# Scores of a head pair in two steps over four PSUM banks instead of three, and the sample's steps moved within the attention stage

## The chip, the cores and the metric

The kernel runs on one core of one Trainium2 chip. The metric is the device time in microseconds (us) of one execution. The engines are TensorE (PE: matmuls and transposes; PEld its weight loads), VectorE (DVE), ScalarE (ACT), GpSimd (POOL) and SyncE (SP), which issues the DMAs.

## The reference

One step of a two-layer encoder for two groups of tokens that share the weights: a prompt of 512 tokens and a sample of 32, so 544 columns in all. A layer projects its input by `W_in`, runs three branches (band attention, retention, a gated recurrence called RG-LRU), merges them by gates, adds a per-layer embedding and ends in a LayerNorm. What the change touches is the attention of the prompt and of the sample, 8 heads of 64. With 512 tokens in chunks of 64 and 8 chunks of look-back every frame sees its own chunk and all before it:

```python
scores = einsum('bcqhd,bckhd->bhcqk', qc * d**-0.5, kp)   # own chunk and 8 before
scores = scores + rel_bias(table, qpos, kpos)              # per head, by clipped distance
scores = where(valid, scores, NEG_INF)
probs  = softmax(scores)
out    = einsum('bhcqk,bckhd->bcqhd', probs, vp)
ya     = out * silu(za)
```

The sample's 32 tokens attend to a cache of 256 keys and to themselves, with the same bias table.

## The kernel before

Activations lie feature by token: 128 features on the partitions, 544 tokens along the row. All projections are streams of blocks: one block is a 128x128 piece of a weight times 544 columns. To keep fp32 accuracy in a faster format each weight and each input is split into a high and a low part (`wh`, `wl`, `xh`, `xl`), and a block (`block`, L248) is three products, each of 288 and 256 columns: six matmuls at L256. The splits are made by ACT (L211) and DVE (L212) from weights that SP loads (L203) into three buffers.

Everything else is done in the gaps between blocks. The order is written out by hand: each side job is a generator; `tick` (L174) runs ahead of each block, issues weight splits that are due (`stream`) and resumes every job whose time has come; a job says by `yield n` in how many blocks it goes on. The table `PACE` (L70) holds these numbers. So a number in `PACE` moves all instructions of a job, on every engine, and each engine then runs its instructions strictly in the order issued.

Attention's part of this, once for each layer:

- `attn_job` (L366) waits until the value transposes, the recurrence's gates and the first key tile are there, and then goes through four pairs of heads. For each pair it loads two bias tables (`bias_loads`, SP, L347), masks a corner on POOL (L379), and starts three steps, eight blocks apart: query tiles (0, 1), then (2,), then (3,).
- `attn_step` (L394) for query tile i has (i + 1) * 128 keys. Two heads of the pair, j = 0 and 1, lie on partitions 0 to 63 and 64 to 127, and their matmuls (L407, 64 rows, three products) write two PSUM banks, `sc`. `exps` (L355) adds the bias and takes the row's maximum on DVE (L357) and exponentials with their sums on ACT (L359); `norm` (L362) divides on DVE (L363, L364). Between these stand `at1` (3), `at1` and `at2` (2) blocks. Then for each head the tile `sx` is transposed on TensorE into the one `tp` bank (L423) and ACT copies it into `PT` (L429); `at3` is 3 blocks.
- `attn_pv` (L436) multiplies the transposed probabilities by the values into the one `pv` bank (L441, 64 columns of the array for each head), and DVE copies the result (L443). It is kept in a list that `flush` (L390) empties: in the next pair's step (0, 1), behind its first transposes, or after the last pair.
- `sample_job` (L454) loads the cache and eight pieces of bias (`sb`, L458) as soon as the last key tile is there, waits 11 blocks, and does the sample's scores (L468), transposes (L481) and values (L494) four, four and three blocks apart.
- At the same time run the recurrence's last scans (DVE L555, POOL L553) in the first pair, the evacuation of new query, key and later-branch tiles from the projections' two `mm` banks (ACT L866, L264, L890; DVE L265, L891), and in the third and fourth pair the rotation of retention's keys: four DMAs on SP copy halves into `swap` (L567, L568), DVE and POOL multiply and add (L570 to L577).

PSUM has eight banks: `mm` takes two buffers of two banks, `sc` two, `tp` and `pv` one each. Small tiles, `sx`, `sb`, `bias` and `swap` among them, share a ring of 14 buffers (`tmp`).

## Time and profile before

| | |
|---|---|
| median of 3 runs | 1309.28 us (1309.03 to 1309.94) |
| the profiled execution's own time | 1310.85 us |
| its span, first to last instruction | 1309.1 us |
| TensorE's mean granted clock | 0.997 |
| TensorE busy | 1291.6 us (99%) |
| DVE, ACT, POOL busy | 718.8, 547.2, 175.8 us |
| score matmuls (L407) on the chain that ended last | 2% of the span |
| values matmuls (L441), transposes (L423) on it | 1% each |

Attention's stage lasts from 96.7 us to some 211 us in the first layer and from 745.4 us to some 860 us in the second. Between 96.7 and 107.2 us DVE is busy for 9.6 of 10.5 us and ACT for 6.6; between 119.6 and 145.3 us DVE for 14.9 of 25.7. A row of the timeline gives start, duration, engine, line, instruction, shapes and count; what the engine waited for ahead of it, if it idled, stands in brackets at its end. Ends of matmuls are modelled, so a cost on TensorE is read from one start to another.

### The profile page before, as it was taken

The page shows a single profiled execution, that of the slowest core. Times are in us where ns is not written, and L with a number is a line of the kernel's source. Part 1 is how long each engine was busy: PE and PEld are TensorE (multiplying, and loading weights), DVE is VectorE, ACT ScalarE, POOL GpSimd, SP SyncE. Part 2 cuts the span into 40 slices and gives each one's busy share as a digit, 9 for nine tenths or more (in the row PEclk, how much of TensorE's full clock was granted, in tenths as well). Part 3 has the DMA queues.
Part 4 walks back from the last instruction along what each step waited for, and adds up shares of the span by engine and source line. Part 5 has one row for each costly group of instructions (what it writes and reads, how often), then busy time and mean ns, then how long its engine had stood idle before and what let it go on. Part 6 is the DMA issues. An engine that isn't in the chain of part 4 may idle for free.

```text
span 1309.1 us, 25085 instructions
## 1 busy us (share of the span) xinstructions
PE 1291.6 (99%) x10550; PEld 1257.1 (96%) x10550; DVE 718.8 (55%) x1272; ACT 547.2 (42%) x1082; POOL 175.8 (13%) x158
## 2 busy tenths in 40 slices
PE   9999999999999999999999999999999999999996
PEld 9999889999999999999989998999999999999996
DVE  5657663573754453465584766626637434434567
ACT  5665544323632233333276655443235322332231
POOL 0110120410101201000032102224001011010000
PEclk9999999999999999999999999999999999999998
DMA  7433522231222222424122345222222222224231
GB/s 263 153 128 100 173 66 82 84 104 49 85 93 82 97 73 90 165 98 146 65 104 79 120 109 166 74 82 82 90 65 81 96 82 84 94 81 166 81 113 69
DMA packets 44609, 134.80 MB, mean 103 GB/s; under 512 B 9488, under 2 KB 11792, under 8 KB 42704
## 3 DMA queue, kind: packets, MB, share of 16 engines
q1 hardware_dynamic: 44496, 133.20, 30.5%
q8 instruction: 83, 1.36, 0.4%
q14 instruction: 30, 0.25, 0.1%
HBM read 117.02 MB, written 11.70 MB: 98 GB/s over the span
## 4 chain that ended last, share of the span: by engine, by line
PE 95%; DVE 3%; DMA 1%; ACT 1%; issue 0%; SPq 0%; POOL 0%; DVEq 0%
PE mm L256 84%; PE sc L407 2%; PE pv L441 1%; PE tp L423 1%; PE tp L334 1%; PE sc L667 1%; PE pv L690 1%; PE pv L522 0%; DVE r L819 0%; PE sc L522 0%; DVE xl L265 0%; PE sc L750 0%; PE sc L603 0%; PE pv L685 0%; DMA raw<-in_W 0%; PE sc L494 0%
## 5 line engine op out<-in xcount | busy, mean ns | idle before, releaser
L256 PE MATMUL mm<-xh,wh 128*128 128x288 f32 x2144 | 455.5, 294 | 0.4 <-ACT xrp L900 0.4
L256 PE MATMUL mm<-xh,wl 128*128 128x288 f32 x2144 | 444.0, 288 | 0.0
L256 PE MATMUL mm<-xl,wh 128*128 128x288 f32 x2144 | 442.7, 288 | 0.0
L212 DVE TENSOR_TENSOR wl<-raw,wh 128x512 fp32r<-128x512 f32 (+1 forms) x354 | 261.3, 756 | 282.2 <-ACT wh L211 278.3
L256 PEld LDWEIGHTS mm<-xh,wh 128*128 128x128 f32 x2144 | 328.4, 189 | 10.8 <-issue 7.5
L256 PEld LDWEIGHTS mm<-xl,wh 128*128 128x128 f32 x2144 | 328.7, 188 | 0.0
L256 PEld LDWEIGHTS mm<-xh,wl 128*128 128x128 f32 x2144 | 328.5, 188 | 0.0
L211 ACT CAST wh<-raw 128x512 fp32r<-128x512 f32 (+1 forms) x354 | 208.2, 614 | 34.2 <-PE mm L256 30.8
L922 ACT ACTIVATE sg<-mm 128x544 f32<-128x544 f32 x48 | 30.0, 625 | 154.0 <-PE mm L256 153.9
L934 POOL TENSOR_TENSOR m<-m,sg 128x544 f32<-128x544 f32 x30 | 46.8, 1561 | 316.7 <-DVE sg L932 316.7
L359 ACT ACTIVATE sx<-sx,sst 128x128 f32<-128x128 f32 (+4 forms) x68 | 38.0, 559 | 65.5 <-DVE sst L357 58.6
L256 PE MATMUL mm<-xh,held 128*128 128x288 f32 (+1 forms) x320 | 64.0, 292 | 0.3 <-ACT ple L942 0.3
L256 PE MATMUL mm<-mh,wh 128*128 128x288 f32 (+1 forms) x256 | 53.0, 288 | 0.0
L256 PE MATMUL mm<-mh,wl 128*128 128x288 f32 (+1 forms) x256 | 53.0, 288 | 0.0
L256 PE MATMUL mm<-ml,wh 128*128 128x288 f32 (+1 forms) x256 | 52.8, 287 | 0.0
L256 PEld LDWEIGHTS mm<-xh,held 128*128 128x128 f32 x320 | 51.3, 188 | 0.6 <-ACT ple L942 0.5
L256 PE MATMUL mm<-xl,held 128*128 128x288 f32 (+1 forms) x160 | 46.3, 290 | 0.6 <-DVE xl L265 0.6
L264 ACT CAST xh<-r 128x544 fp32r<-128x544 f32 (+2 forms) x32 | 17.0, 532 | 68.3 <-DVE r L952 64.1
L932 DVE TENSOR_TENSOR sg<-mm,sg 128x544 f32<-128x544 f32 x32 | 23.2, 725 | 37.1 <-PE mm L256 37.1
L913 ACT ACTIVATE z<-mm 128x544 f32<-128x544 f32 x24 | 15.0, 626 | 59.6 <-PE mm L256 59.6
L571 POOL TENSOR_TENSOR swap<-swap,cst 128x544 f32<-128x544 f32 x16 | 25.3, 1579 | 108.4 <-DMA swap<-QB 32.1
L256 PEld LDWEIGHTS mm<-mh,wh 128*128 128x128 f32 x256 | 39.4, 188 | 0.0
(251 smaller groups left out, 1785.2 us busy)
## 6 DMA issues: line engine op xcount, KB each, us to landing
raw<-in_W SPq DMA_DIRECT2D x189, 512.0 KB, 3.3
pled<-ple SPq DMA_DIRECT2D x4, 1088.0 KB, 9.0
ple<-pled SPq DMA_DIRECT2D x4, 1088.0 KB, 6.8
bias<-in_RB SPq DMA_DIRECT2D x16, 256.0 KB, 3.8
x<-in_xT SPq DMA_DIRECT2D x4, 544.0 KB, 9.3
o_v<-VA SPq DMA_DIRECT2D x2, 1088.0 KB, 4.6
o_k<-KT SPq DMA_DIRECT2D x2, 1088.0 KB, 5.1
swap<-KB SPq DMA_DIRECT2D x32, 68.0 KB, 2.0
```

The source lines that it names most:

```text
L211: S.copy(h[:, k:k + step], t)
L212: V.tensor_tensor(lo[:, k:k + step], t, h[:, k:k + step].bitcast(F32), SUB)
L256: T.matmul(ps[:, MM0 + a:MM0 + b], lhsT=w[:, n % 4, :], rhs=x[:, a:b], start=first and i == 0, stop=last and i == 2)
L264: S.copy(h, src)
L334: T.transpose(tp[:rows, t * 128:(t + 1) * 128], src[:, t, c0:c0 + rows], ident)
L359: S.activation(x, x, AF.Exp, bias=s[:, 0:1], scale=-1.0, accum_out=s[:, 1:2])
L407: T.matmul(scs[j][:, o:o + n], lhsT=q_[r, p, i * 128:i * 128 + 128], rhs=k_[r, p, :n], start=k == 0, stop=k == 2)
L571: G.tensor_tensor(sw, sw, cst[:, C_SIN:C_SIN + N], MUL)
L913: S.activation(z, pv, AF.Sigmoid)
L922: S.activation(sg, pv, AF.Sigmoid)
L932: V.tensor_tensor(sg, pv, sg, MUL)
L934: (V if kind == "bB" and t == 7 else G).tensor_tensor(m, m, sg, ADD)
```

## The change

The steps of a pair are (3, 1) and (2, 0), 11 and 13 blocks apart (24 blocks a pair as before). Step (3, 1) is the wide one: the scores of query tile 3 go to the two `sc` banks, those of tile 1 to the `tp` bank (first head) and the `pv` bank (second head). Its probabilities lie in three `sx` tiles, one for each head's 512 columns and one that both heads share with 256 columns each, so it has three groups of four transposes. Step (2, 0) keeps both of its tiles in the `sc` banks, 384 + 128 columns, and has two groups of four. The values of the pair before are flushed behind the wide step's first transposes; the next pair's bias loads stand at the second step. After the last step 3 blocks pass (`attn_end`), where it was 9. The sample's bias pieces are loaded 12 blocks later than its cache, and its first scores 12 blocks after that.

```diff
-    "va0": 5, "va": 3, "step": 8, "attn_end": 9, ... "sample": 11, ...
+    "va0": 5, "va": 3, "step": (11, 13), "attn_end": 3, ... "sample": 12, ...
@@ attn_job
-                for qs in ((0, 1), (2,), (3,)):
-                    if qs[0] == 2 and p < 3:
+                for n, qs in enumerate(((3, 1), (2, 0))):
+                    if n and p < 3:
                         bias_loads(p + 1)
                     add(attn_step(p, qs))
-                    yield PACE["step"]
+                    yield PACE["step"][n]
@@ attn_step
-            scs, xs, todo = [psum("sc") for _ in range(2)], [], []
-            o = 0
+            wide = qs[0] == 3
+            scs, xs = [psum("sc") for _ in range(2)], [tmp("sx", (128, 512)) for _ in range(2)]
+            at_ = {(qs[0], j): (scs[j], xs[j], 0) for j in range(2)}
+            if wide:
+                x = tmp("sx", (128, 512))
+                at_.update({(qs[1], j): (psum(("tp", "pv")[j]), x, 256 * j) for j in range(2)})
+            else:
+                at_.update({(qs[1], j): (scs[j], xs[j], 128 * (qs[0] + 1)) for j in range(2)})
...
-                        T.matmul(scs[j][:, o:o + n], lhsT=q_[r, p, i * 128:i * 128 + 128], rhs=k_[r, p, :n],
+                        sc, x, o = at_[i, j]
+                        o *= not wide
+                        T.matmul(sc[:, o:o + n], lhsT=q_[r, p, i * 128:i * 128 + 128], rhs=k_[r, p, :n],
                                  start=k == 0, stop=k == 2)
...
-            for j in range(2):
+            for x in xs + ([at_[1, 0][1]] if wide else []):
                 tp = psum("tp")
-                for c in range(0, o, 128):
-                    T.transpose(tp[:, c:c + 128], xs[j][:, c:c + 128], ident)
-                if j == 0 and qs[0] == 0:
+                mine = sorted((o, i, j) for (i, j), (_, y, o) in at_.items() if y is x)
+                end = mine[-1][0] + 128 * (mine[-1][1] + 1)
+                for c in range(0, end, 128):
+                    T.transpose(tp[:, c:c + 128], x[:, c:c + 128], ident)
+                if wide and x is xs[0]:
                     flush()
-                for i in qs:
+                for c, i, j in mine:
                     copy("p%d" % j)(env["PT"][j][:, :i + 1, i * 128:i * 128 + 128],
                                     tp[:, c:c + 128 * (i + 1)].rearrange("p (a b) -> p a b", b=128))
-                    c += 128 * (i + 1)
+                if not wide and x is xs[1]:
+                    env["pvs"].append(lambda: attn_pv(p))
                 yield PACE["at3"]
-            if qs[-1] == 3:
-                env["pvs"].append(lambda: attn_pv(p))
@@ sample_job
             ks, vc = sample_loads()
+            while "ya" not in env:
+                yield 2
+            yield PACE["sample"]
             sb = [tmp("sb", (128, PAST + NS)) for _ in range(2)]
             for h in range(8):
                 Q.dma_start(out=sb[h % 2][32 * (h // 2):32 * (h // 2) + 32],
                             in_=RB[l, h, 0:NS, 128:128 + PAST + NS])
-            while "ya" not in env:
-                yield 2
-            yield PACE["sample"]
+            yield 12
```

How this moves instructions is shown at three places. TensorE, the first step of the first pair of heads: `sc`, `tp` and `pv` ahead of the arrow are the banks written, `KTh`, `KTl`, `QTh`, `QTl` the high and low parts of keys and queries. Before:

```order
684 L256 MATMUL mm<-xh,wl 128x256
685 L407 MATMUL sc<-KTh,QTh 128x128 x2
686 L407 MATMUL sc<-KTh,QTl 128x128 x2
687 L407 MATMUL sc<-KTl,QTh 128x128 x2
688 L407 MATMUL sc<-KTh,QTh 128x256 x2
689 L407 MATMUL sc<-KTh,QTl 128x256 x2
690 L407 MATMUL sc<-KTl,QTh 128x256 x2
691 L256 MATMUL mm<-xh,wh 128x288
```

and now:

```order
684 L256 MATMUL mm<-xh,wl 128x256
685 L414 MATMUL sc<-KTh,QTh 128x512 x2
686 L414 MATMUL sc<-KTh,QTl 128x512 x2
687 L414 MATMUL sc<-KTl,QTh 128x512 x2
688 L414 MATMUL tp<-KTh,QTh 128x256
689 L414 MATMUL pv<-KTh,QTh 128x256
690 L414 MATMUL tp<-KTh,QTl 128x256
691 L414 MATMUL pv<-KTh,QTl 128x256
692 L414 MATMUL tp<-KTl,QTh 128x256
693 L414 MATMUL pv<-KTl,QTh 128x256
694 L256 MATMUL mm<-xh,wh 128x288
```

The step holds 512 + 256 columns a head in place of 128 + 256, and the smaller group is written to the other two banks.

TensorE again, where the values of the first pair are multiplied, in the second pair's time. Before:

```order
900 L256 MATMUL mm<-xh,wl 128x256
901 L423 MATMUL tp<-cst,sx 128x128 x3
902 L441 MATMUL pv<-PT,vatok 64x512 x2
903 L441 MATMUL pv<-PT,vatok 64x384 x2
904 L441 MATMUL pv<-PT,vatok 64x256 x2
905 L441 MATMUL pv<-PT,vatok 64x128 x2
906 L407 MATMUL sc<-KTh,QTh 128x384 x2
907 L407 MATMUL sc<-KTh,QTl 128x384 x2
908 L407 MATMUL sc<-KTl,QTh 128x384 x2
909 L256 MATMUL mm<-xh,wh 128x288
```

and now:

```order
905 L256 MATMUL mm<-xh,wl 128x256
906 L434 MATMUL tp<-cst,sx 128x128 x4
907 L450 MATMUL pv<-PT,vatok 64x512 x2
908 L450 MATMUL pv<-PT,vatok 64x384 x2
909 L450 MATMUL pv<-PT,vatok 64x256 x2
910 L450 MATMUL pv<-PT,vatok 64x128 x2
911 L256 MATMUL mm<-xh,wh 128x288
```

Step (2,)'s scores stood right behind the values; now projection blocks do, and the scores of step (2, 0) come three blocks later, behind the wide step's second transposes.

ACT, from the exponentials of the first pair's first step to its copies of transposed probabilities. Before:

```order
118 L359 ACT_TABLE_LOAD
119 L359 ACTIVATE sx,sst<-sx,sst 128x128
120 L359 ACTIVATE sx,sst<-sx,sst 128x256
121 L211 CAST wh<-raw 128x512
122 L359 ACTIVATE sx,sst<-sx,sst 128x128
123 L359 ACTIVATE sx,sst<-sx,sst 128x256
124 L866 COPY KT<-mm 128x544
125 L264 CAST KTh<-KT 128x544
126 L211 CAST wh<-raw 128x512
127 L429 COPY PT<-tp 128x128
128 L429 COPY PT<-tp 128x2x128
129 L359 ACTIVATE sx,sst<-sx,sst 128x384
```

and now:

```order
118 L359 ACT_TABLE_LOAD
119 L359 ACTIVATE sx,sst<-sx,sst 128x512
120 L359 ACTIVATE sx,sst<-sx,sst 128x256
121 L211 CAST wh<-raw 128x512
122 L359 ACTIVATE sx,sst<-sx,sst 128x512
123 L359 ACTIVATE sx,sst<-sx,sst 128x256
124 L876 COPY KT<-mm 128x544
125 L264 CAST KTh<-KT 128x544
126 L211 CAST wh<-raw 128x512
127 L439 COPY PT<-tp 128x4x128
128 L211 CAST wh<-raw 128x512
129 L439 COPY PT<-tp 128x4x128
```

The order of kinds is the same up to the first copy; two exponentials have grown from 128 to 512 columns, and one copy of 512 stands for two of 128 and 256. DVE's order in this stretch changes in the same way. On SP the eight `sb` loads of a layer, which stood ahead of the first key tile's four `swap` copies, now stand behind these and the next weight load, ahead of the second key tile's four; the last pair's `bias` loads, which stood ahead of those four, now stand behind them.

More of the change, by code (lines that the diff above doesn't have):

```diff
@@ L395, in attn_step @@
             QTh, QTl, KTh, KTl = (env[k] for k in ("QTh", "QTl", "KTh", "KTl"))
-            scs, xs, todo = [psum("sc") for _ in range(2)], [], []
-            o = 0
+            wide = qs[0] == 3
[6 more added lines that the diff above has]
+                at_.update({(qs[1], j): (scs[j], xs[j], 128 * (qs[0] + 1)) for j in range(2)})
             now = [], []
-            for j in range(2):
-                xs.append(tmp("sx", (128, 512)))
             for i in qs:
@@ L406, in attn_step @@
                         r = slice(64 * j, 64 * j + 64)
-                        T.matmul(scs[j][:, o:o + n], lhsT=q_[r, p, i * 128:i * 128 + 128], rhs=k_[r, p, :n],
+                        sc, x, o = at_[i, j]
+                        o *= not wide
+                        T.matmul(sc[:, o:o + n], lhsT=q_[r, p, i * 128:i * 128 + 128], rhs=k_[r, p, :n],
                                  start=k == 0, stop=k == 2)
                 for j in range(2):
-                    now[j].append((xs[j][:, o:o + n], scs[j][:, o:o + n], env["bias", p, j][:, 512 - n:]))
-                o += n
+                    sc, x, o = at_[i, j]
+                    c = 0 if wide else o
+                    now[j].append((x[:, o:o + n], sc[:, c:c + n], env["bias", p, j][:, 512 - n:]))
+            todo = []
             for j in range(2):
@@ L419, in attn_step @@
             yield PACE["at2"]
-            for j in range(2):
+            for x in xs + ([at_[1, 0][1]] if wide else []):
                 tp = psum("tp")
-                for c in range(0, o, 128):
-                    T.transpose(tp[:, c:c + 128], xs[j][:, c:c + 128], ident)
-                if j == 0 and qs[0] == 0:
+                mine = sorted((o, i, j) for (i, j), (_, y, o) in at_.items() if y is x)
[3 more added lines that the diff above has]
+                if wide and x is xs[0]:
                     flush()
-                c = 0
-                for i in qs:
+                for c, i, j in mine:
                     copy("p%d" % j)(env["PT"][j][:, :i + 1, i * 128:i * 128 + 128],
                                     tp[:, c:c + 128 * (i + 1)].rearrange("p (a b) -> p a b", b=128))
-                    c += 128 * (i + 1)
+                if not wide and x is xs[1]:
+                    env["pvs"].append(lambda: attn_pv(p))
                 yield PACE["at3"]
-            if qs[-1] == 3:
-                env["pvs"].append(lambda: attn_pv(p))
         def attn_pv(p):
```

2 rows, old and new, of the table PACE are left out of this document.

## The prediction

> **What bounds the kernel now.** I read the page first, then the chain, then what TensorE waited for. In the page, busy times:
>
> ```profile
> PE 1291.6 (99%) x10550; PEld 1257.1 (96%) x10550; DVE 718.8 (55%) x1272; ACT 547.2 (42%) x1082; POOL 175.8 (13%) x158
> ...
> PE 95%; DVE 3%; DMA 1%; ACT 1%; issue 0%; SPq 0%; POOL 0%; DVEq 0%
> ```
>
> TensorE is busy from end to end, and the chain that ended last runs 95% through it. So only two things can move the end: what TensorE itself spends on the attention steps, and time in which it is made to wait. Its waits, first and last of 8 groups:
>
> ```profile
> PE tp L750 <- DVE r L968: 2.0, 2, 1.4
> ...
> PE mm L256 <- ACT phl L264: 0.2, 1, 0.2
> ```
>
> The eight add up to 7.8 us, and none of them lies in attention (95 to 211 us, and 744 to 860 us for the second layer). No wait is there to be removed; the change can gain only in TensorE's own time.
>
> What a score step costs is read from start to start, since ends are modelled. A row of the timeline is start, duration, instruction. First the step (0,1), then steps (2,) and (3,), each behind three transposes, and between them three transposes alone:
>
> ```profile
> 96.40 0.41 PE L256 MATMUL mm<-xh,wl 128*128 128x288 f32 x2
> ...
> 97.02 0.27 PE L407 MATMUL sc<-KTl,QTh 64*128 64x128 f32 x2
> 97.13 0.34 PE L407 MATMUL sc<-KTh,QTh 64*128 64x256 f32 x2
> 97.30 0.28 PE L407 MATMUL sc<-KTh,QTl 64*128 64x256 f32 x2
> 97.42 0.28 PE L407 MATMUL sc<-KTl,QTh 64*128 64x256 f32 x2
> ...
> 97.99 0.41 PE L256 MATMUL mm<-xl,wh 128*128 128x288 f32 x2
> ...
> 103.51 0.42 PE L256 MATMUL mm<-xh,wl 128*128 128x288 f32 x2
> ...
> 105.27 0.41 PE L256 MATMUL mm<-xl,wh 128*128 128x288 f32 x2
> ...
> 107.01 0.41 PE L256 MATMUL mm<-xh,wl 128*128 128x288 f32 x2
> ...
> 107.84 0.41 PE L256 MATMUL mm<-xl,wh 128*128 128x288 f32 x2
> ...
> 111.12 0.42 PE L256 MATMUL mm<-xh,wl 128*128 128x288 f32 x2
> ...
> 113.06 0.41 PE L256 MATMUL mm<-xl,wh 128*128 128x288 f32 x2
> ```
>
> From 97.99 to 103.51 stand 22 pairs of projection matmuls: 5.52 / 22 = 0.251 us a pair, 0.753 us a block of three. Each stretch above holds two such pairs, so 0.50 is taken off. (0,1): 1.59 - 0.50 = 1.09. Three transposes: 0.83 - 0.50 = 0.33, or 0.11 each. (2,): 1.76 - 0.50 - 0.33 = 0.93. (3,): 1.94 - 0.50 - 0.33 = 1.11. A pair of heads pays 3.13 us for scores.
>
> **The scores, two steps for three.** The matmuls stay the same in number and shape; groups are joined. A group that comes second in a step costs only its own starts: for 256 columns 0.17 (97.13 to 97.30), 0.12, and 0.12 again; for 128 columns 0.17 and twice 0.11 (97.02 to 97.13). So step (3,1) is 1.11 + 0.41 = 1.52, step (2,0) is 0.93 + 0.39 = 1.32, together 2.84: 0.29 less in the first pair of heads. If the first start of a joined group is no dearer than its others, it is 0.40 less; if a group in another bank saves nothing, zero. I take 0.29, the rows' own value.
>
> In the later pairs the old step (2,) stood directly behind the probabilities-times-values matmuls, and in the new order projection matmuls follow those. What the neighbourhood was worth:
>
> ```profile
> 126.91 0.42 PE L256 MATMUL mm<-xh,wl 128*128 128x288 f32 x2
> ...
> 130.97 0.42 PE L256 MATMUL mm<-xl,wh 128*128 128x288 f32 x2
> ...
> 207.78 0.41 PE L256 MATMUL mm<-xh,wl 128*128 128x288 f32 x2
> ...
> 210.79 0.41 PE L256 MATMUL mm<-xl,wh 128*128 128x288 f32 x2
> ```
>
> The first stretch holds three transposes, the pv group and step (2,): 4.06 - 0.50 - 0.33 = 3.23. The second holds the pv group alone: 3.01 - 0.50 = 2.51. Side by side the score step cost 0.72 instead of 0.93, and this 0.21 is given up in three of four pairs. A layer saves 4 x 0.29 - 3 x 0.21 = 0.53 us, two layers **1.1 us** (with 0.40 and otherwise the same 1.9; with zero it loses 1.3).
>
> By the Trainium skill, TensorEngine Tiling (Array Packing), Key Properties, it is the change of tiling mode, not of tile, that drains the engine; its page TensorE: Matmul & The Clock Gate, Step-by-step, puts a drain at about 128 cycles, 0.053 us as an estimate. The new order has ten changes of mode fewer, which would be worth 0.5 us, where the rows give 0.1 a change and 1.1 in all; that the gain goes by changes of mode agrees with the rows, the page's price is half of theirs.
>
> Transposes stay 20 a pair, in five groups instead of six; at 0.11 each and nothing by group this is zero. The sample's matmuls are the same, spread anew: zero, or 0.1 a layer either way for one score group that now stands before transposes.
>
> **The new wait.** The wide step's first two transpose groups stand three blocks apart with nothing but blocks between, and share the one tp bank. ACT must empty it in that time. In the first pair of each layer ACT and DVE are late, because DVE still scans for the recurrence:
>
> ```profile
> 99.34 1.36 POOL L553 TENSOR_TENSOR lru_r<-lru_r,lru_i 128x544 f32<-128x544 f32 x1
> 99.41 2.37 DVE L555 TENSOR_TENSOR_SCAN lru_i<-lru_a,lru_r 128x512 f32<-128x512 f32 x1
> ...
> 102.65 0.29 DVE L364 TENSOR_SCALAR sx<-sx,sst 128x128 f32<-128x128 f32 x1
> ...
> 103.31 0.28 DVE L357 CUSTOM_DVE_ANT_0 sx<-sc,bias 128x128 f32<-128x128 f32 x1
> ...
> 104.04 0.49 ACT L359 ACTIVATE sx<-sx,sst 128x256 f32<-128x256 f32 x1
> ...
> 106.23 0.53 ACT L429 COPY PT<-tp 128x128 f32<-128x128 f32 x2
> ...
> 107.26 0.49 PE L423 MATMUL tp<-cst,sx 128*128 128x128 f32 x3
> ...
> 114.36 0.68 DVE L357 CUSTOM_DVE_ANT_0 sx<-sc,bias 128x512 f32<-128x512 f32 x1
> ...
> 115.08 0.72 ACT L359 ACTIVATE sx<-sx,sst 128x512 f32<-128x512 f32 x1 [0.99 <-DVE sst L357]
> ...
> 115.80 0.60 ACT L211 CAST wh<-raw 128x512 fp32r<-128x512 f32 x1
> ...
> 119.47 0.49 DVE L364 TENSOR_SCALAR sx<-sx,sst 128x512 f32<-128x512 f32 x1
> ...
> 120.85 0.58 ACT L429 COPY PT<-tp 128x512 f32<-128x512 f32 x1
> ...
> 747.74 1.37 POOL L553 TENSOR_TENSOR lru_r<-lru_r,lru_i 128x544 f32<-128x544 f32 x1
> 748.10 2.08 DVE L555 TENSOR_TENSOR_SCAN lru_i<-lru_a,lru_r 128x512 f32<-128x512 f32 x1
> ...
> 754.63 0.53 ACT L429 COPY PT<-tp 128x128 f32<-128x128 f32 x2
> ...
> 755.94 0.49 PE L423 MATMUL tp<-cst,sx 128*128 128x128 f32 x3
> ```
>
> Old order: ACT's copies end at 106.76 and the next group starts at 107.26, 0.50 to spare. New order, step by step. The first head's score instructions take about 0.4 longer (512 columns for 128), but the scan behind them ended 1.08 and 1.07 us after POOL's end in the two layers, however long after POOL's start it began; so its end stays. The norm grows by 0.49 - 0.29 = 0.20: the second head's 512 scores start at 103.51. Its exponential starts 0.72 later (114.36 to 115.08), at 104.23, and the next one 0.72 after that, at 104.95, where 104.04 stood: 0.91 late. Key copy, cast and weight cast follow as before, so the PT copy starts at 106.23 + 0.91 = 107.14 and, with 512 columns, ends at 107.72. TensorE meanwhile comes earlier: 107.26 less three transposes and step (2,) between (0.33 + 0.93), plus the longer first step (0.43) and four transposes (0.44): 106.87. It **waits 0.85 us**. In the second layer the copy ends at 754.63 + 0.91 + 0.58 = 756.12 and TensorE comes at 755.55: 0.57. Together **1.4 us**. If the scan's end moved with its start this would be 2.2; if ACT kept the old times, zero. I take 1.4, since the end held in both layers.
>
> Later places have cover. In pairs two to four the pv group (2.3 us) lies between the first two transpose groups. The wide step's own matmuls into the tp bank start two blocks and the 512 columns (1.5 + 0.7) after the narrow step's last transposes, whose copies need some 0.8.
>
> **Moved DMAs.** The sample's eight bias loads now stand on SP ahead of the second key tile's four swaps, and one pair's bias loads behind them:
>
> ```profile
> 139.77 5.86 SPq L458 DMA_DIRECT2D sb<-in_RB  x8
> ...
> 151.14 0.35 SPq L203 DMA_DIRECT2D raw<-in_W  x1
> ...
> 155.91 0.51 SPq L567 DMA_DIRECT2D swap<-KB  x1
> ...
> 162.56 1.61 DVE L570 TENSOR_TENSOR KB<-KB,cst 128x544 f32<-128x544 f32 x1
> ```
>
> Behind that raw load they end at 151.5 + 5.9 = 157.4, so the swaps leave up to 1.5 us late. Behind the waiting DVE rotation (L570) are queued the narrow step's norms, for which transposes wait that stand eight blocks (6 us) after its scores. That covers it; uncovered it costs one rotation, 1.6 us a layer. Weight loads keep their times. I take zero.
>
> **Sum.** -1.1 + 1.4 = +0.3 us. The profiled execution, 1310.85 us with a span of 1309.1, would be 1311.15 (span 1309.4). It lay 1.57 above the runs' median of 1309.28, so that median becomes **1309.6**. The likeliest case's own range, gain 1.0 to 1.9 and wait 0.8 to 2.2, is 1308.2 to 1310.5.
>
> **Rivals.** *No wait*: ACT is in time and the gain stands, 1309.28 - 1.1 = 1308.2 (1307.4 with 1.9). For it speaks the old 0.50 to spare, against it the 0.91. *The tp bank is late everywhere*: if in pairs two to four the copies end as late as in the first (over 2.2 us after the transposes, from where it decides), the wide step waits inside its scores. The first pair's copies ended 2.5 us after theirs (103.51 + 0.25 + the 0.49 of such a group, 104.25, to 106.76), 512 columns would add 0.2: 0.5 each in six places, 1309.6 + 3.0 = 1312.6, slower. Against it: without the scan nothing holds ACT up there. It goes by the Trainium skill's Perfetto Trace Analysis, Matmuls, which asks that independent groups rotate through different banks so that emptying overlaps. *Joining saves a step's whole fixed cost*: 1.09 less three starts of 0.11 and three of 0.12 leaves 0.40; eight of these, the neighbourhood kept and no wait: -3.2, 1306.1, faster. Against it: the 0.17 of the second group and the 3.23.
>
> **Chances.** Forecast 0.58, no wait 0.22, late everywhere 0.12, whole fixed cost 0.05, other small differences 0.03. A measurement of this kernel can tell about 0.2%, 2.6 us. Only "late everywhere" and a tail of lost cover lie above it (0.14), only the last rival and a little of "no wait" below (0.06); 0.80 is no change. The range, 1307.4 to 1312.0, holds the first two cases with their bounds and leaves out most of the other two.
>
> **What would show it.** Right: in the first pair of each layer a TensorE wait of 0.5 to 1.0 us at the second transpose group, on ACT's PT copy; steps of 1.52 and 1.32 us; pv followed by blocks at 2.5. Wrong: no wait there, or one at the wide step's tp matmuls, at the sample's scores, or on DVE for KB behind a swap; a joined group that starts at other intervals in another bank.

## The result, and the profile after

The change made the kernel slower: 1319.14 us median of 6 runs (1316.42 to 1320.59) against 1308.49 (1307.13 to 1309.94), ratio 1.0074, 95% interval 1.0063 to 1.0085. The forecast was 1309.6 with a range to 1312.0, and it gave 0.80 to no change that a measurement can tell. The measured median lies 7.1 us above the range, and the loss of 0.74% is clear of the noise. The profiled execution took 1319.89 us with a span of 1318.0, 8.9 more than before.

The page of the changed kernel, busy times and the chain that ended last:

```profile
PE 1295.1 (98%) x10550; PEld 1260.1 (96%) x10550; DVE 709.7 (54%) x1272; ACT 542.7 (41%) x1082; POOL 174.9 (13%) x158
...
PE 86%; DVE 7%; ACT 4%; issue 2%; DMA 1%; DVEq 0%; POOL 0%; SPq 0%; ACTq 0%
```

TensorE's share of the chain fell from 95 to 86%: DVE and ACT now set the pace in places. What TensorE waited for (us in all, times, longest), the three groups that did not exist before:

```profile
PE tp L434 <- ACT PT L494: 4.4, 2, 2.3
...
PE tp L434 <- ACT PT L439: 1.3, 2, 0.7
...
PE tp L334 <- ACT VB L876: 0.7, 2, 0.4
```

The second was forecast; the first, which is the largest, was not. L494 is the sample's copy of its transposed probabilities. The place is the fourth pair's wide step. Rows of the timeline (start, duration, instruction, idle time before it and who ended it):

```profile
172.47 0.41 PE L256 MATMUL mm<-xh,wl 128*128 128x288 f32 x2
172.81 0.50 PE L414 MATMUL sc<-KTh,QTh 64*128 64x512 f32 x2
...
174.43 0.41 PE L256 MATMUL mm<-xl,wh 128*128 128x288 f32 x2
...
178.56 1.36 POOL L581 TENSOR_TENSOR swap<-swap,cst 128x544 f32<-128x544 f32 x1
178.60 1.60 DVE L364 TENSOR_SCALAR sx<-sx,sst 128x512 f32<-128x512 f32 x1
179.02 0.49 PE L491 MATMUL tp<-cst,sx 128*128 128x128 f32 x3
180.61 0.41 PE L256 MATMUL mm<-xh,wl 128*128 128x288 f32 x2
180.78 0.69 DVE L357 CUSTOM_DVE_ANT_0 sx<-sc,bias 128x512 f32<-128x512 f32 x1
181.56 0.72 ACT L359 ACTIVATE sx<-sx,sst 128x512 f32<-128x512 f32 x1 [3.64 <-issue]
182.28 0.49 ACT L359 ACTIVATE sx<-sx,sst 128x256 f32<-128x256 f32 x1
182.78 0.35 ACT L493 COPY PT<-tp 128x256 f32<-128x256 f32 x1
183.03 0.25 ACT L494 COPY PT<-tp 32x128 f32<-32x128 f32 x1
183.33 0.66 PE L434 MATMUL tp<-cst,sx 128*128 128x128 f32 x4 [2.31 <-ACT PT L494]
183.92 4.07 PE L450 MATMUL pv<-PT,vatok 128*64 128x512 f32 x16
187.91 0.52 PE L256 MATMUL mm<-xh,wh 128*128 128x288 f32 x2
```

Read it from the bottom. The wide step's first transposes start at 183.33, 2.31 us after TensorE was free for them, when ACT has emptied the one tp bank (183.28). In that bank lay the sample's second transposes (179.02). ACT could have copied them out at once, since it sat idle for 3.64 us, but it runs its instructions in order, and ahead of the copy stood the exponentials of the wide step's second head (181.56 to 182.77), which waited for DVE's scores of that head (180.78 to 181.47; the row of the exponential names no releaser, but it starts 0.09 us after them), which stood behind DVE's normalisation of the first head: 1.60 us for 512 columns, as long as POOL was multiplying. Then pv took 4.07 us where it took 2.3 before. The windows of the same trace say why (columns: stretch, length, busy PE, PEld, DVE, ACT, POOL, granted clock, DMA share, GB/s):

```profile
184.00:185.00 1.00, 1.00 (x4) 0.35 (x6) 0.00 (x0) 0.00 (x0) 0.00 (x0) 0.64 0.00 0
185.00:186.00 1.00, 1.00 (x5) 0.25 (x3) 0.00 (x0) 0.00 (x0) 0.00 (x0) 0.50 0.00 0
...
187.00:188.00 1.00, 1.00 (x9) 0.57 (x5) 0.00 (x0) 0.00 (x0) 0.00 (x0) 0.65 0.00 0
188.00:189.00 1.00, 1.00 (x10) 0.85 (x12) 0.00 (x0) 0.00 (x0) 0.00 (x0) 1.00 0.00 0
```

The granted TensorE clock is halved from 184.28 to 187.70, for 3.4 us, right behind the stall; work done at half speed for 3.4 us costs 1.7. The second layer shows the same: a wait of 2.12, then the half clock from 836.23 to 839.64.

Because the traces hold the same 9038 matmuls into `mm` in the same order (9024 of the projections, and 14 with zeros at the program's start), two kernels can be laid side by side by block number, six matmuls to a block: the time from the start of one block to the start of another, minus the same in the kernel before. This is my own sum from the traces, in us; blocks 106 to 131 hold the first pair, 131 to 235 the other pairs and the transposes after them, 235 to 366 most of the retention stage, and the same 752 blocks later for layer 2. The rows below the first are the kernels of the experiments:

```
                      layer 1                    layer 2            all the
                106-131 131-235 235-366    106-131 131-235 235-366   rest
the change        1.32    3.56    0.58       1.27    3.31    0.71   -1.80
steps only        1.41   -0.22    1.77       1.26   -0.23    1.88   -2.82
early loads       1.45    3.31    0.60       1.17    2.78    0.70   -2.53
fill              1.17    1.87    0.58       1.19    1.65    0.75   -3.60
other bank        1.39   -0.18    0.58       1.14   -0.41    0.69   -3.34
end 5             1.54    3.56    0.58       1.25    3.31    0.71   -2.88
end 9             1.81    2.97   -0.03       1.32    2.70    0.00   -0.89
rotation on DVE   1.31    0.99    1.26       1.27    1.03    1.38   -2.92
own gap           1.50   -1.69   -0.04       1.24   -1.71    0.01   -0.45
gap, first pair   1.45   -1.70   -0.05       0.98   -1.71    0.02   -1.93
the same again    1.39   -1.73   -0.04       0.80   -1.72    0.02   -3.39
third on DVE      1.97   -1.70   -0.06       1.75   -1.72    0.02   -2.21
```

The change costs 5.5 us in layer 1 and 5.3 in layer 2. "All the rest" is the start of the program, the stretch between the layers and the end, in which no row of the change stands; it differs by 1.5 us between two traces of one kernel ("gap, first pair" and "the same again"), so the six columns are what is compared. Nearly all of it lies in two places. The first 30 blocks end at 27.0 to 29.6 us, according to when TensorE leaves for good the half rate at which it starts: in the kernel before's trace its matmuls start 0.24 us apart until 10.55 us and 0.13 us apart behind that, and in the thirteen traces the switch to the full rate comes at 9.8 to 11.1 us five times and at 4.0 to 6.7 us eight times. And the turn between the layers, blocks 700 to 740, is 0.7 to 1.6 us shorter in every trace than in the kernel before's one trace.

A layer's 5.5 us are made of these, each measured from start to start against the same instructions where nothing waits:

- the joined scores: -1.3 (below)
- first pair, second transposes behind ACT's copy: +0.9 (0.8 in layer 2)
- fourth pair, stall and half clock: +4.2 (4.0)
- fourth pair, narrow step behind the sample's values: +0.45
- first transposes of VB: +0.6
- blocks near 282, weights late: +0.6 (0.7)

The sum is 5.45 in layer 1 and 5.25 in layer 2. The narrow step's share is read from rows, and no run takes it away by itself: the sample's values lie in one of the two score banks until DVE copies them out, which ends at 193.76, and of the first two score matmuls (193.37) the second starts only at 193.82.

```profile
192.83 0.60 PE L434 MATMUL tp<-cst,sx 128*128 128x128 f32 x4
...
193.37 0.89 PE L414 MATMUL sc<-KTh,QTh 64*128 64x384 f32 x2
193.48 0.28 DVE L508 COPY ya<-sc 128x128 f32<-128x128 f32 x1
...
193.82 0.61 PE L414 MATMUL sc<-KTh,QTl 64*128 64x384 f32 x2
```

### The profile page after: what moved, and what is told of

It is laid out like the page before. It is cut to its first block, busy times and chain, and to the rows that moved or that the text cites. A ratio compares the mean times of both kernels' runs of the same rounds, so it can differ in the third digit from the quotient of the medians.

```text
span 1318.0 us, 25056 instructions
## 1 busy us (share of the span) xinstructions
PE 1295.1 (98%) x10550; PEld 1260.1 (96%) x10550; DVE 709.7 (54%) x1272; ACT 542.7 (41%) x1082; POOL 174.9 (13%) x158
## 3 DMA queue, kind: packets, MB, share of 16 engines
q8 instruction: 83, 1.36, 0.4%
## 4 chain that ended last, share of the span: by engine, by line
PE 86%; DVE 7%; ACT 4%; issue 2%; DMA 1%; DVEq 0%; POOL 0%; SPq 0%; ACTq 0%
PE mm L256 77%; PE pv L450 2%; PE tp L434 1%; DVE wl L212 1%; PE sc L414 1%; ACT wh L211 1%; PE sc L677 1%; PE tp L334 1%; PE pv L700 1%; DVE lru_i L565 1%; ACT sx L359 0%; PE pv L532 0%; PE sc L532 0%; PE sc L760 0%; PE sc L613 0%
## 5 line engine op out<-in xcount | busy, mean ns | idle before, releaser
L359 ACT ACTIVATE sx<-sx,sst 128x512 f32<-128x512 f32 (+2 forms) x68 | 37.7, 557 | 49.3 <-DVE sst L357 39.7
L439 ACT COPY PT<-tp 128x384 f32<-128x384 f32 (+2 forms) x64 | 24.9, 428 | 36.5 <-PE tp L434 34.7
```

The costliest lines, as they stand in the source:

```text
L359: S.activation(x, x, AF.Exp, bias=s[:, 0:1], scale=-1.0, accum_out=s[:, 1:2])
L439: copy("p%d" % j)(env["PT"][j][:, :i + 1, i * 128:i * 128 + 128], tp[:, c:c + 128 * (i + 1)].rearrange("p (a b) -> p a b", b=128))
```

## The experiments

Theory A, formed from these rows: the loss is the meeting of the sample's second transposes with the fourth wide step in one bank, made longer by ACT's and DVE's order, and dearer by the clock. Against it stand: B, that a step over four banks loses by itself; C, that the bias loads moved on SP make the rotation late; D to F, that a wait which is taken away comes back elsewhere. Ratios are against the kernel before, run on the same chip, with 95% intervals.

**The two-step scores with the sample where it was.** The lines of the sample are as before the change, the rest is the change:

```diff
-    "at1": 3, "at2": 2, "at3": 3, "sample": 12, "sa1": 4, "sa2": 4,
+    "at1": 3, "at2": 2, "at3": 3, "sample": 11, "sa1": 4, "sa2": 4,
...
             ks, vc = sample_loads()
+            sb = [tmp("sb", (128, PAST + NS)) for _ in range(2)]
+            for h in range(8):
+                Q.dma_start(out=sb[h % 2][32 * (h // 2):32 * (h // 2) + 32],
+                            in_=RB[l, h, 0:NS, 128:128 + PAST + NS])
             while "ya" not in env:
                 yield 2
             yield PACE["sample"]
-            sb = [tmp("sb", (128, PAST + NS)) for _ in range(2)]
-            for h in range(8):
-                Q.dma_start(out=sb[h % 2][32 * (h // 2):32 * (h // 2) + 32],
-                            in_=RB[l, h, 0:NS, 128:128 + PAST + NS])
-            yield 12
```

> The two-step scores with the sample's steps and bias loads where they stood before the change. Theory A (the loss of 10 us is a collision of the sample's transposes with the fourth wide step): the 2.1 to 2.3 us waits at the fourth pair's wide transposes and the half clock behind them are gone, in both layers. The first pair's wait (0.7 and 0.6) and the one at the first VB transposes (0.4) stay. New small waits appear where the sample now stands: about 0.5 at its second score group (bank read by DVE 6.5 us after the third wide step's start) and about 1.2 where its transposes stand directly ahead of the third wide step's last ones in the one tp bank. Sum per layer 1.7 + 0.75 + 0.6 - 1.25 = +1.8: about 1312 us, clock 0.997 in all runs. Theory B (the wide step's four banks are themselves the loss): 1317 to 1320, with TensorE waits of 2 us or more left at a wide step.

Measured: 1314.20 us, ratio 1.0048 (1.0035 to 1.0062), clock 0.996 to 0.997 in all runs. The 2 us waits are gone, and with them the half clock; B falls. The waits of TensorE that stand in their place:

```profile
PE mm L256 <- ACT wh L211: 2.1, 3, 0.9
...
PE tp L434 <- ACT PT L493: 1.2, 2, 0.6
```

The second is the expected one where the sample's transposes stand directly ahead of the wide step's. The first was not expected: in the retention stage the weights come late by 1.8 us a layer (the column 235-366), for which the expectation had no term. The expected 1.2 at the tp bank is 0.6 a layer in this list (0.8 from start to start), and the expected 0.5 at the second score group did not come. Together that is 0.9 us more a layer than expected, most of the 2 us by which 1312 missed.

**The loads early.** Only the eight loads go back ahead of the sample's first wait, its steps stay late.

```diff
             ks, vc = sample_loads()
+            sb = [tmp("sb", (128, PAST + NS)) for _ in range(2)]
+            for h in range(8):
+                Q.dma_start(out=sb[h % 2][32 * (h // 2):32 * (h // 2) + 32],
+                            in_=RB[l, h, 0:NS, 128:128 + PAST + NS])
             while "ya" not in env:
                 yield 2
             yield PACE["sample"]
-            sb = [tmp("sb", (128, PAST + NS)) for _ in range(2)]
-            for h in range(8):
-                Q.dma_start(out=sb[h % 2][32 * (h // 2):32 * (h // 2) + 32],
-                            in_=RB[l, h, 0:NS, 128:128 + PAST + NS])
             yield 12
```

> As the change, but the sample's eight bias loads are issued at the old place, early; its other steps stay late. Theory A (tp bank, ACT's queue): nothing changes around 180 us, waits of 2.0 to 2.4 us on the sample's PT copy stay, 1316.5 to 1320.5. Theory C (the loads on SP make the rotation's swaps late, and with them DVE's scores for the second head): the wait falls below 1 us, the half clock is gone, about 1311.

Measured: 1319.67 us, ratio 1.0088 (1.0074 to 1.0102). The waits stay, 2.10 us in each layer; C falls. This trace also shows something that the change's own could not, since here the two layers differ. Layer 1, then layer 2, the wait and pv:

```profile
181.93 0.65 PE L434 MATMUL tp<-cst,sx 128*128 128x128 f32 x4 [2.10 <-ACT PT L494]
182.51 3.97 PE L450 MATMUL pv<-PT,vatok 128*64 128x512 f32 x16
...
835.81 0.66 PE L434 MATMUL tp<-cst,sx 128*128 128x128 f32 x4 [2.10 <-ACT PT L494]
836.39 2.38 PE L450 MATMUL pv<-PT,vatok 128*64 128x512 f32 x16
```

and the granted clock behind each, in the windows (eighth figure, ahead of the DMA share):

```profile
183.50:187.00 3.50, 3.50 (x18) 1.78 (x15) 0.00 (x0) 0.00 (x0) 0.00 (x0) 0.57 0.00 0
...
836.00:840.00 4.00, 4.00 (x34) 2.40 (x33) 0.04 (x1) 0.00 (x0) 0.00 (x0) 1.00 0.02 4
```

The same wait to the hundredth, once with the half clock behind it and once without. So a stall of 2.1 us may halve the clock or not, and the changed kernel's own six runs fit that: two at 1316.4 and 1316.5 with a mean clock of 0.997, one at 1318.4 with 0.996, three at 1319.9 to 1320.6 with 0.994 and 0.995; steps of about 1.8 us. That these are none, one and two halved stretches is read from the sizes; only the profiled run shows it. What tells the two layers apart stands in the last section.

**Work in place of the stall.** Eighteen matmuls of zeros ahead of the fourth wide step's transposes; their results go to a free score bank, taking one turn of the two, and are not read; all else is the change.

```diff
             yield PACE["at2"]
+            if wide and p == 3:
+                fill = psum("sc")
+                for _ in range(18):
+                    T.matmul(fill[:, :H2], lhsT=zero[:, :128], rhs=zero, start=True, stop=True)
```

> As the change, but 18 matmuls of zeros (272 columns, about 0.126 us each, 2.3 us together) stand ahead of the fourth wide step's transposes, whose results nobody reads: TensorE works through the time in which it would wait. Theory A1 (standing still for over 2 us is what halves the granted clock for 3.4 us): the pv group behind takes 2.3 us and not 4.0, clock 0.997 in every run, 1315 to 1317 although work was added. Theory A2 (the clock falls for another reason, or the pv group is slow by itself): pv still 4.0, 1319 to 1321.

Measured: 1315.75 us, ratio 1.0057 (1.0044 to 1.0069), below the change's 1.0074 though work was added (the intervals overlap, so the rows carry this, not the times); clock 0.996 to 0.998 in all five runs.

```profile
178.95 2.42 PE L432 MATMUL sc<-zero 128*128 128x272 f32 x18
181.43 0.66 PE L438 MATMUL tp<-cst,sx 128*128 128x128 f32 x4
182.01 2.37 PE L454 MATMUL pv<-PT,vatok 128*64 128x512 f32 x16
```

The transposes start as late as ever, but pv takes 2.37. In the table the column 131-235 falls by 1.69 and 1.66 against the change: that is the half clock's price, apart from the wait. A1 holds.

**The sample's second transposes in another bank.**

```diff
-                tp = psum("tp")
+                tp = psum(("tp", "sc")[j])
```

> As the change, in all places, but the sample's second group of transposes goes to a bank of the scores' pair instead of the tp bank. Theory A (the fourth wide step's transposes wait for nothing but that one bank, which ACT empties behind the second head's exponentials): the waits of 2.3 and 2.1 us are gone though ACT's copies stay as late as they were, pv takes 2.4, no half clock; 4.2 + 4.0 less: about 1311. Theory E (TensorE would have had to wait there anyhow, for DVE's late normalisation of the first head or for the pv bank): a wait of over 1 us with another name stays, 1314 or more.

Measured: 1311.48 us, ratio 1.0021 (1.0012 to 1.0030).

```profile
177.32 0.49 PE L491 MATMUL sc<-cst,sx 128*128 128x128 f32 x3
179.16 0.60 PE L434 MATMUL tp<-cst,sx 128*128 128x128 f32 x4
180.18 2.37 PE L450 MATMUL pv<-PT,vatok 128*64 128x512 f32 x16 [0.42 <-DVE sst L357]
...
181.33 0.25 ACT L494 COPY PT<-sc 32x128 f32<-32x128 f32 x1
```

ACT's copy now ends 1.4 us after pv has begun, and nobody waits for it. What is left of theory E is 0.42 us: pv needs a bank that holds the second head's scores, and would have waited that long anyhow. 3.7 us a layer are gone (the column 131-235) of the 4.2 and 4.0 reckoned. The rule of the Trainium skill that the prediction set against the change (Perfetto Trace Analysis, Matmuls: let independent groups rotate through different banks, so that emptying overlaps) is what this run shows, at a place that the prediction had not looked at.

**POOL's part.** The three multiplications of a rotation that POOL does go to DVE.

```diff
-            G.tensor_tensor(sw, sw, cst[:, C_SIN:C_SIN + N], MUL)
+            V.tensor_tensor(sw, sw, cst[:, C_SIN:C_SIN + N], MUL)
...
-            G.tensor_tensor(e, e, bc(w, [[0, 4], [1, 128]]), MUL)
-            G.tensor_tensor(a[:, NP:], a[:, NP:], w[:, :NS], MUL)
+            V.tensor_tensor(e, e, bc(w, [[0, 4], [1, 128]]), MUL)
+            V.tensor_tensor(a[:, NP:], a[:, NP:], w[:, :NS], MUL)
```

> As the change, but the three multiplications of a key or query tile's rotation that POOL does are done by DVE. In the change's fourth pair DVE's normalisation of the first head (512 columns) took 1.60 us while POOL multiplied, and 0.49 in other places. Theory P (POOL's work beside it is what makes it slow): 0.49 in the fourth pair too, in both layers, though DVE now has about 1.5 us more of its own there. Theory Q (it is slow for another reason): 1.6 stays. For the wait at the fourth wide step's transposes theory A expects no cure either way: 1.5 to 3 us, since the rows that POOL gives up stand in the same queue of DVE.

Measured, one run: 1315.24 us, beside 1309.72 for the kernel before.

```profile
177.65 0.49 DVE L364 TENSOR_SCALAR sx<-sx,sst 128x512 f32<-128x512 f32 x1
...
180.75 0.25 ACT L494 COPY PT<-tp 32x128 f32<-32x128 f32 x1
181.06 0.66 PE L434 MATMUL tp<-cst,sx 128*128 128x128 f32 x4 [0.73 <-ACT PT L494]
181.64 2.37 PE L450 MATMUL pv<-PT,vatok 128*64 128x512 f32 x16
```

P holds: 0.49 and not 1.60. But the expectation for the wait was wrong: it fell from 2.31 to 0.73, though DVE took over POOL's rows, and the half clock went with it. So of the change's wait of 2.31 us, 1.6 is what POOL cost DVE, net of the rows that DVE took over, and without those 1.6 the clock's 1.7 did not come either. Wait and half clock together hang on the bank, as the run before showed. The column 131-235 is 2.3 to 2.6 us better than the change's and not 3.3, since another wait on ACT's copies, 0.7 from start to start, came at block 177; and in the retention stage the weights are late by 1.3 us a layer, not 0.6. One run of each kernel is too little to read the time by; the rows are what counts here.

**The end of attention.** Two tries to start the retention stage where it started before: with five blocks behind the last score step, and then with nine as before the change.

```diff
-    "attn_end": 3, "at1": 3,
+    "attn_end": 5, "at1": 3,
```

```diff
-    "attn_end": 3, "at1": 3,
+    "attn_end": 9, "at1": 3,
```

> As the change, but five blocks instead of three behind the last score step, so that the retention stage starts where it started before. The waits of 4 us in the fourth pair stay. Theory A: the wait at the first VB transposes (0.6 a layer from start to start) and one of 0.65 a layer in the projection blocks of the retention stage go: 2.5 less than the change, 1314 to 1318. Theory F (they come from the late fourth pair, not from the earlier start): both stay, no difference.

> As the change, but nine blocks behind the last score step as before the change, so that the last pv group stands at block 211 and the retention stage starts at block 212 and not 210. Theory A (two small waits a layer come from the retention stage's start two blocks earlier): the wait of 0.6 at the first VB transposes and the one of 0.65 in the blocks near 282 go, 2.5 us less than the change from start to start at equal blocks; the waits of the fourth pair stay: 1314 to 1318. Theory F (they follow from the late fourth pair): both stay.

With 5: 1318.80 us, ratio 1.0073 (1.0057 to 1.0089). The edit did not reach its aim: the last pv moved from block 205 to 207, but the first transposes of VB still stood at block 210, so this run says nothing for A or F. With 9 they stand at block 212: 1318.02 us, ratio 1.0064 (1.0051 to 1.0078); the wait on VB is not in its list any more, and the column 235-366 is -0.03 and 0.00. Theory A holds, F falls, at 0.6 to 0.7 for each of the two waits in each layer. It is the rows that show this: the interval overlaps the change's, and 1318.02 is at the upper end of what was expected. What is late there is plain in the change's rows, where the last tile of VB is emptied while its transposes wait:

```profile
214.03 0.61 ACT L876 COPY VB<-mm 128x544 f32<-128x544 f32 x1 [6.89 <-PE mm L256]
...
214.70 0.33 PE L334 MATMUL tp<-cst,VB 128*128 128x128 f32 x1 [0.37 <-ACT VB L876]
```

**A gap of its own for the sample.** The fourth pair starts eight blocks later and the sample's steps are tighter, so that they all end ahead of the fourth wide step.

```diff
-    "attn_end": 3, "at1": 3, "at2": 2, "at3": 3, "sample": 12, "sa1": 4, "sa2": 4,
+    "attn_end": 1, "at1": 3, "at2": 2, "at3": 3, "sample": 12, "sa1": 3, "sa2": 3,
...
-                    yield PACE["step"][n]
+                    yield PACE["step"][n] + 8 * (n and p == 2)
```

> As the change, but the fourth pair starts eight blocks later and the sample's steps are three blocks tighter, so that they all stand between the third pair's last transposes and the fourth wide step; the last pv group stands where it stood before. Theory A: no wait at the fourth wide step's transposes, no half clock, no wait at the first VB transposes; what is left is the first pair's wait of 0.7 and 0.6 and the gain of about 1.25 a layer: 1308.5 - 2.5 + 1.3 = 1307.3, clock 0.997. Theory B: the wide steps lose wherever the sample stands, 1315 or more.

Measured: 1308.44 us, ratio 0.9998 (0.9989 to 1.0007). All waits in attention are gone but the first pair's, 1.5 us in two places:

```profile
PE tp L434 <- ACT PT L439: 1.5, 2, 0.9
```

The column 131-235 is -1.7 in both layers. B falls again.

**The first pair.** With the gap, the second transpose group of the first pair two blocks later:

```diff
-                yield PACE["at3"]
+                yield PACE["at3"] + 2 * (wide and p == 0 and x is xs[0])
```

> As the own gap for the sample, and in the first pair the second transpose group stands five blocks behind the first instead of three, apart from the narrow step. Theory A: the wait of 0.9 and 0.6 us on ACT's PT copy goes, nothing takes its place (perhaps 0.1 for one more change between transposes, scores and blocks). Attention then takes 1.1 us less than before the change in each layer: 2.2 us off the kernel before, ratio 0.998 to 0.999. Theory D (the wait only moves on to the next transposes): as the own gap alone, ratio 0.9995 to 1.0005.

> The kernel with the sample's own gap and five blocks behind the first pair's first transposes, once more, beside the next two on one chip. In its trace the first pair's wait had moved to the narrow step's first transposes (0.8 and 0.35 us instead of 0.9 and 0.6). If the 0.9985 measured for it is the trace's own difference (attention 1.0 us less than before the change, both layers together) and not chance: ratio 0.9985 to 0.9995. If it was chance: 1.000.

Measured: 1306.53 us, ratio 0.9985 (0.9976 to 0.9994); the same kernel on another chip 1306.18, ratio 0.9980 (0.9971 to 0.9989). Faster than the kernel before, both times. But theory D was right about the wait: it moved to the narrow step's first transposes, which now start behind the third group's copy on ACT.

```profile
115.29 0.66 PE L434 MATMUL tp<-cst,sx 128*128 128x128 f32 x4 [0.81 <-ACT PT L439]
```

It is 0.81 there and 0.35 in layer 2, and by the table its first pairs are only 0.05 to 0.11 us shorter than with the own gap alone in layer 1, and 0.26 to 0.44 in layer 2. Attention is 1.0 to 1.3 us shorter than before the change; the medians differ by 2.0 and 2.6, the fastest runs by 1.7 and 1.5. How the rest is shared stays open, but the traces show two places for it. One is the start of the program: the two traces of this very kernel differ there by 1.7 us, since TensorE leaves its half rate at 9.79 us in one and at 5.65 us in the other. The other is a wait that stands in the one trace of the kernel before, at the turn between the layers, and is shorter or absent in every other trace:

```profile
PE sc L750 <- DVE r L968: 1.7, 1, 1.7
```

Whether the kernel before has this wait in every run, and how often it starts late, its one trace cannot say.

**The first pair once more.** Its third group one block earlier, and copied out by DVE:

```diff
-                    copy("p%d" % j)(env["PT"][j][:, :i + 1, i * 128:i * 128 + 128],
+                    (V.tensor_copy if wide and p == 0 and x is not xs[0] and x is not xs[1] else copy("p%d" % j))(env["PT"][j][:, :i + 1, i * 128:i * 128 + 128],
...
-                yield PACE["at3"] + 2 * (wide and p == 0 and x is xs[0])
+                yield PACE["at3"] + (wide and p == 0) * ((x is xs[0]) * 2 - (x is xs[1]))
```

> As the one above, but in the first pair the third transpose group comes one block earlier, and DVE instead of ACT copies it out. Theory A (each of these waits is ACT's queue alone): the wait at the narrow step's first transposes falls to 0.5 or less in layer 1 and to nothing in layer 2, the attention is 0.6 us shorter than above. Theory D (the first pair has no slack anywhere: the wait moves once more, to DVE behind its QTl row): no difference from the one above.

Measured: 1308.76 us, ratio 0.9997 (0.9988 to 1.0006), beside 0.9980 on the same chip: 2.6 us slower, of which the two first pairs are 0.6 and 0.9.

```profile
PE tp L434 <- DVE sst L363: 2.5, 2, 1.4
```

Theory D is right in kind, though it expected no difference: the wait moved once more, to DVE, and grew. In these two tries the first pair had no slack on either engine.

## Why the prediction was wrong

**What bounds the kernel** stood: TensorE before and after, and no wait in attention to be removed. Every microsecond lost is TensorE waiting or at half clock.

**The scores, two steps for three.** The mechanism was right, the sizes were not: "step (3,1) is 1.11 + 0.41 = 1.52, step (2,0) is 0.93 + 0.39 = 1.32". The wide step takes 172.47 to 174.43 less two pairs, 1.96 - 0.50 = 1.46. The narrow step, behind four transposes of 0.44:

```profile
132.69 0.41 PE L256 MATMUL mm<-xh,wl 128*128 128x288 f32 x2
...
134.10 0.22 PE L414 MATMUL sc<-KTh,QTh 64*128 64x128 f32 x2
134.16 0.28 PE L414 MATMUL sc<-KTh,QTl 64*128 64x128 f32 x2
...
134.83 0.42 PE L256 MATMUL mm<-xl,wh 128*128 128x288 f32 x2
```

2.14 - 0.50 - 0.44 = 1.20. The first start of a joined group is no dearer than the others but cheaper (134.10 to 134.16: 0.06, where 0.17 was taken). With these two steps a pair saves 0.47 and not 0.29, and four pairs less the prediction's 0.63 for the neighbourhood come to 1.25 us a layer and not 0.53; the own gap shows the same: its layers are 0.23 and 0.46 us shorter than before with first-pair waits of 1.09 and 0.80 from start to start in them, 1.3 without. So "1.1 us" for both layers should have been 2.6. By changes of tiling mode (ten fewer) that is 0.26 a change, and not all of it need be the change of mode. The Trainium skill's drain (TensorE: Matmul & The Clock Gate, Step-by-step) gave an estimate of 0.053, a fifth of what the rows show.

**The new wait** stood, in place, in cause and nearly in size: 0.85 and 0.57 forecast, 0.91 and 0.84 from start to start (0.70 and 0.6 in the list of waits). What it was built on held too: in the first layer the scan again ended 1.08 us after POOL's end.

**"Later places have cover"** is the step that failed, together with "The sample's matmuls are the same, spread anew: zero". The first was said of pairs two to four, and it holds for two and three: no wait in either. The fourth pair was not looked at by itself. There the sample's two transpose groups stand inside the cover, between the wide step's scores and its transposes, in the same single bank, and their copies stand on ACT behind an exponential that waits for DVE. A moved step was priced by its own instructions, and not by the bank it holds and the queue its release stands in. That cost 4.2 and 4.0 us, of which 1.7 each is a halved clock, for which the prediction had no term.

**Two more terms were missing.** The score bank that the sample's values hold ahead of the narrow step (0.45 a layer), and `attn_end`, 9 made 3, which lets the retention stage start two blocks earlier, on a tile that has just been finished and on weights that are late (1.2 to 1.3 a layer). The diff showed that number, and the prediction did not price it.

**Moved DMAs: zero** stood; with the loads early the waits were still there, at 2.10.

**The rivals.** "The tp bank is late everywhere" had the right bank and the wrong places: it asked whether the wide step's own copies are late in pairs two to four, and they are not. "No wait" and "joining saves a step's whole fixed cost" fell, though the second was nearer on the gain: it put the saving on 3.2, the forecast on 1.1, and it is 2.6. The sum with what was measured is -2.6 + 1.7 + 8.2 + 0.9 + 2.5 = +10.7 us, and the difference of the medians is 10.65. That these agree so closely is luck: the sum holds both halved stretches and the median run perhaps one or two, and the two profiled executions differ by 8.9, mostly since the turn between the layers took 1.6 longer in the kernel before's. The range went wrong because the largest term had no place in it.

## What to carry to other kernels

Price a step that is moved by what it holds: which bank, until which instruction of which in-order queue has run, and who needs that bank meanwhile; look at the one place where the new neighbours differ from the repeating pattern, not only at the pattern. In a kernel bound by TensorE, a stall of two microseconds is not priced by its length, since the clock behind it may be halved. And when a wait is taken away by spacing, look in the next trace where it went: here it moved twice, and grew the second time.

## What the runs showed of the hardware

**The clock after a stall.** A stall of 2.1 to 2.3 us was followed by 3.4 us at half clock in both layers of the change and of both end kernels, and in one of two layers with the loads early; and not where zeros were multiplied in the stall or where the stall was shorter (0.73 with the rotation on DVE, 1.35 in the last variant's first pair, 1.4 near 660 us in every trace). Only at the program's end, where TensorE runs out of work, does the clock fall in every trace, and in two traces it falls once in the first 8 us.

The clock records of the traces say more. The time between two of its changes is always a whole multiple of 3.41 us: in the change 190 of them from 187.70 to 836.23, with the loads early 329 from 186.54 to 1309.52. So the clock changes on a grid that the program does not set. Laid on this grid, each of the seven stalls that were punished lies within one period; the change's first, 181.02 to 183.33, lies in the period from 180.87 to 184.28, at whose end the clock falls. The stall that was spared, 833.71 to 835.81, is cut by the grid at 835.07, into 1.36 us in one period and 0.74 in the next. So what counts seems to be the idle time within one period: 2.10 us and more were punished seven times of seven, 1.4 us never in the middle of the program. Where between these the limit lies, no run shows, and one spared stall is little to go by. The Trainium skill (TensorE: Matmul & The Clock Gate, The HAM clock gate) tells of a free-running window of about 3.4 us in which activity is watched. The length of the half clock and the grid agree with that. The Trainium skill's section on HAM oscillation, on the same page, gives as the rule no gaps over about 3.4 us; here 2.1 were enough when they fell within one period, so the measurement decides for the shorter.

**POOL beside DVE.** A row of 512 columns that takes 0.49 us on DVE took 1.60 beside a multiplication of POOL's that started with it, and ended 0.28 us after that (180.20 against 179.92); without them it took 0.49 at the same place. The kernel before has such a row too, 1.75 us at 169.59 beside the same multiplication, and there TensorE waited for nothing. The Trainium skill (SBUF — State Buffer, SBUF: two separate sides) describes a port pair that DVE and GpSimd share under a lock held for a whole instruction, so that the loser waits; it says so of some kinds of DVE instruction, and whether this row is one of them no run shows. The rows agree with that: moving POOL's multiplications to DVE made DVE's queue faster, not slower, at this place.
